# First layer of a two-layer backbone: queries kept in DRAM as rows of channels with both parts of a token block side by side, one store per tile, and requests spaced one tile apart

## The chip, the cores and the metric

The kernel runs on one NeuronCore of a Trainium2 chip. A core has five engines that run their own instruction streams in order and meet at semaphores: PE (TensorE, matrix products; its weight loads, PEld, overlap the products), DVE (VectorE), ACT (ScalarE), POOL (GpSimd) and SP (SyncE, which here issues nearly all transfers). Data lives in DRAM (HBM), in the on-chip memory of 128 partitions, and in PSUM, eight banks into which PE writes. The metric is the device time of one execution in microseconds (us); lower is better.

## The reference, cut to what matters

A backbone of two layers over 1024 latent tokens and 256 context tokens of width 1024. Each layer computes `x += gate * mixer(adaLN(RMSNorm(x)))`; layer 0 mixes by windowed attention with grouped heads (16 query heads, 4 key/value heads, head size 64), layer 1 by multi-head latent attention. What the change touches is the projection of layer 0 and where its queries are kept:

```python
def adaln(cond, w, bias):
    m = jax.nn.silu(cond) @ w + bias
    return jnp.split(m, 3, axis=-1)

def project(h):
    q, k, v, g = jnp.split(h @ w_in, [A_WIDTH, A_WIDTH + A_KV_WIDTH, A_WIDTH + 2 * A_KV_WIDTH], axis=-1)
    ...

qx, kx, vx, gx = project(hx)
qc, kc, vc, gc = project(hc)
qx = apply_rope(qx, cos, sin)
kx = apply_rope(kx, cos, sin)
...
ox = lax.map(attend_block, (qb, kw, vw, mask))
...
yx = (ox * jax.nn.silu(gx)) @ w_out
```

All tensors are fp32. The vectors of adaLN (shift, scale and gate of each layer, for latent and for context tokens) come from products of one conditioning vector with a matrix of 1024 x 3072 per layer.

## The kernel before

**Two parts per number.** An fp32 product is made of three faster ones: every operand is kept as a high part, which ACT makes by a cast (`split`, L120), and a low part, the difference, which DVE or POOL makes (L121); `mm3` (L123–127) issues high x high, low x high, high x low. So L125, L126 and L127 in the profile are the three products of one step.

**The projection of layer 0** (about 100 to 357 us) goes over ten blocks of 256 columns of `a_w_in`, in the order of `blocks`: 0 is V, made earlier; 1, 3, 5 and 6 are queries, 7 is the keys, 2, 4, 8 and 9 are gates. The list `order` (L678–679) has for each of the blocks 1 to 7 one tile of the 256 context tokens (`gp` 0; 48 matmuls of 128x256) and four tiles of 512 latent tokens by 128 columns (`gp` 1 and 2, `c` 0 and 1; 24 matmuls of 128x512); blocks 8 and 9 take the latent tiles first and the context tiles last. One entry of `order` is an *item*. The loop is L747–771. In each item it first calls `fetch` for the block after the current one, then `next_item`, which runs whatever `later(d, fn)` has put off until this item, then some steps of adaLN, and then `proj_t`.

**Weights.** `fetch` (L269–271) calls `load_w` (L222–228): four pieces of 256 KB on SP's queue, each into one of three staging buffers (`stg`), then split by ACT (L120) and POOL (L121) into one of two weight buffers. A fourth piece can be loaded only when the first has been split. The loads of a piece may run far ahead of its split, since nothing but the staging buffer holds them.

**adaLN beside the products.** The remaining adaLN products don't go through PE as matrix products but through DVE: `ada_vec` loads a matrix in 64 pieces of 128x512 (L341, a ring of four buffers), and adds each, scaled by one column of conditioning per partition, to one or two accumulators (L360 for the first piece of a job, L362 for the others; 112 operations in eight jobs). A finished job goes to `ada_sum`: PE sums over partitions (L373), ACT copies the row out of PSUM (L377) or DVE adds a bias (L379). One item later `ada_end` turns the row into columns by four PE transposes (L392), which DVE reads (L167, L170), or stores the row (L385). The loop draws `steps(ada_steps, n)` operations at each item: 2 at a latent tile and 5 at a context tile of a query or key block, 6 at a tile of a gate block, and whatever is left at block 8.

**A query tile** (`proj_t`, L422–492). A latent tile is rotated: DVE multiplies by the cosines (L468) and shuffles (L469), POOL multiplies by the sines (L470) and adds (L472). The rest is done one item later (`rest`): ACT's cast (L120) and DVE's difference (L121) into a staging buffer, then four stores (L487) to `q0_d`, one for each half of the partitions and each part. A context tile has no rotation: cast, difference, four stores (L461). A gate tile is one activation on ACT (L443) and one store (L446, context L448).

**The readback.** `q0_d` is `[4, 64, 2, NT, 512]`: group of four heads, channel, part (high, low), block of 128 tokens, and 512 numbers for four heads of 128 tokens. Attention runs in 40 units of one token block and one group; `prep_q` (L541–548) loads a unit's queries with two transfers (L545), the same rows to both halves of the partitions, in runs of 2 KB. `score` then multiplies by the keys (L569, L570), DVE takes the maximum (L576), ACT the exponential (L579). Other loads on the same queue are the gates (L553) and the output weights (L670).

**Order.** Instructions of one engine run in the order in which the build's scheduler placed them, which follows the program's order and its own estimate of when each can run. So moving a call in the program can move other instructions on the same engine.

Of the kernel before, what the change touches and what calls it, by code (L numbers as in the profile page):

```python
# [9 lines left out]
F32 = mybir.dt.float32  # L10
# [12 lines left out]
NT = TOK // 128  # L23
# [36 lines left out]
def kernel(ctx: ExitStack, tc: tile.TileContext, t, out, dbg=None):  # L60
# [11 lines left out]

    q0_d = dpool.tile([4, 64, 2, NT, 512], F32, name="q0_d")
    g0_d = dpool.tile([8, 128, TOK], F32, name="g0_d")
# [238 lines left out]

    due = []
    item = [0]

    def later(d, fn):
        due.append((item[0] + d, fn))

    def next_item():  # L320
        item[0] += 1
        todo = [x for x in due if x[0] <= item[0]]
        due[:] = [x for x in due if x[0] > item[0]]
        for _, fn in todo:
            fn()

    def ada_vec():
# [18 lines left out]
        for a, cb in jobs:  # L346
# [9 lines left out]
            for k in range(8):  # L356
                w = ws.pop(i)
                for c in range(nw):
                    if k == 0:
                        nc.vector.tensor_scalar_mul(accs[c], w, sc[:, k, c : c + 1])  # L360
                    else:
                        nc.vector.scalar_tensor_tensor(accs[c], w, sc[:, k, c : c + 1], accs[c], ALU.mult, ALU.add)  # L362
# [59 lines left out]
    def proj_t(bi, gp, c):  # L422
        W, c0 = wt[bi], blocks[bi]
        ps = PB[:, 4, :] if (bi, gp) == (9, 0) else pss()
        for cc in (c,) if gp else range(2):
            if gp:
                o = shp(ps, 2, 256)
            elif c0 < 1024:
                o = shp(ps, 2, 2, 128)[:, :, cc, :]
            else:  # L430
                o = ps[:, cc * 256 : cc * 256 + 256]
            for k in range(8):
                if gp:
                    m = [hw[gp][:, :, s, k, :] for s in range(2)]
                elif c0 < 1024:
                    m = [shp(hT[0][:, s, k, :], 2, 128) for s in range(2)]
                else:
                    m = [hT[0][:, s, k, :] for s in range(2)]
# [11 lines left out]
        if gp == 0:  # L450
# [23 lines left out]
        def rest():  # L474
            q = shp(qst.next(), 2, 512)
            if c0 == 1024:
                for e in range(2):
                    es = slice(64 * e, 64 * e + 64)
# [3 lines left out]
                return  # L482
            split(q[:, 0].bitcast(F32R), q[:, 1].bitcast(F32R), a)
            for e in range(2):
                for s in range(2):
                    o0 = e * 256 + c * 128
                    load(  # L487
                        out=q0_d[c0 // 256, :, s, t0 // 128 : t0 // 128 + 4, o0 : o0 + 128],
                        in_=shp(q[64 * e : 64 * e + 64, s], 4, 128),
                    )  # L490

# [15 lines left out]
    ogr = Ring(R, [64, 72], 2048)  # L507
    qtb = [r_at(o, 2, 4, 128) for o in (72, 76, 80, 84, 108)]
    ptr = Ring(R, [88, 92, 96, 100, 104], 1024)
# [17 lines left out]
    class UnitA:  # L527
# [13 lines left out]
        def prep_q(self):  # L541
            i = 4 * ORDER.index(self.ti) + self.g
            self.qT = qtb[i if i < 2 else 2 + (i - 2) % 3]
            for b in range(2):
                load(  # L545
                    out=self.qT[64 * b : 64 * b + 64].bitcast(F32).rearrange("p s h n -> p s (h n)"),
                    in_=q0_d[self.g, :, :, self.ti, :],
                )

# [6 lines left out]
        def score(self, h):  # L556
            g, qT = self.g, self.qT
            P = Pr.next()
            hq = 2 * (h % 2) + h // 2
            self.Ps.append(P)  # L560
# [6 lines left out]
            for i, (po, n, ko, mo) in enumerate(parts):  # L567
                S = pss3()[:, 0:n]
                nc.tensor.matmul(S, qT[:, 0, hq, :], kT[:, g, ko : ko + n], start=True, stop=False)  # L569
                nc.tensor.matmul(S, qT[:, 1, hq, :], kT[:, g, ko : ko + n], start=False, stop=True)  # L570
                prev = sk if mx is None else mx
# [174 lines left out]
    started = {0, 1}  # L746
    for bi, gp, c in order:  # L747
        if bi + 1 < 10 and bi + 1 not in started:
            started.add(bi + 1)
            fetch(bi + 1)  # L750
        next_item()
        steps(ada_steps, 200 if (bi, gp) == (8, 0) else 6 if blocks[bi] >= 1536 else 2 if gp else 5)
        if (bi, gp, c) == (9, 2, 0):
# [16 lines left out]
        if bi >= 8 and gp != 1:  # L770
            for _ in range(2):
                next(wo_fill, None)

    units[1].score(0)
    units[1].score(1)
# [756 lines left out]
```

## Time and profile before

| | us |
|---|---|
| median of three runs | 1643.87 |
| lowest, highest of them | 1639.46, 1645.17 |
| the profiled execution, its own time | 1647.77 |
| its span, first to last instruction | 1645.9 |
| PE busy | 1587.9 |
| DVE, ACT, POOL busy | 964.1, 825.2, 792.5 |
| layer-0 projection after V (blocks 1 to 9) | about 100 to 357 |
| layer-0 attention | about 357 to 750 |
| layer 1 | the rest |

The rows of a timeline are: start in us, length in us, engine, source line, operation, what is written and what is read, how many instructions are joined in the row, and in brackets the idle time before it and what ended that idle time. SPq is SP issuing transfers: its length is that of issuing, not of the transfer. A row of the waits view is: engine, tile and line that waited, what it waited for, then the microseconds in total, how often, and the longest.

### The profile page before, as it was taken

The numbers are of one execution on the slowest core, as the hardware profiler recorded it, in microseconds if no ns is written. First come the engines' busy times: TensorE is split into PE (matmuls) and PEld (weight loads), VectorE is DVE, ScalarE is ACT, GpSimd is POOL, SyncE is SP. The second block draws the span as 40 slices with busy tenths as digits, with TensorE's granted clock in tenths as the row PEclk, the third lists the DMA queues.
The fourth block names the chain that finished last, engine by engine and source line by source line (L and its number), as shares of the span: only waits on it lengthen the run. The fifth ranks groups of instructions, "written<-read, shape, count | busy, mean of one in ns | idle before, by whom it ended". The sixth has DMA issues, their size and how long they took to land.

```text
span 1645.9 us, 23722 instructions
## 1 busy us (share of the span) xinstructions
PE 1587.9 (96%) x8156; PEld 1215.5 (74%) x8156; DVE 964.1 (59%) x1972; ACT 825.2 (50%) x1779; POOL 792.5 (48%) x776
## 2 busy tenths in 40 slices
PE   6899999999999999998999999999999999999998
PEld 2687778887878888878887887566756756666687
DVE  1797853539888888869454015655555455455354
ACT  3622112249777777777333334555555555555421
POOL 1444426224453333345254423686676777668510
PEclk9899999999999999999999999999999999999999
DMA  8557665364343333334127713111111111122151
GB/s 280 165 154 204 180 206 141 94 178 124 93 119 94 91 90 90 90 113 160 52 90 251 222 61 103 61 55 33 39 40 34 45 40 35 49 77 69 47 160 65
DMA packets 127202, 176.75 MB, mean 107 GB/s; under 512 B 11100, under 2 KB 69084, under 8 KB 127080
## 3 DMA queue, kind: packets, MB, share of 16 engines
q1 hardware_dynamic: 124920, 171.12, 34.4%
q10 hardware_dynamic: 2160, 4.11, 0.8%
q8 instruction: 64, 1.05, 0.3%
q14 instruction: 58, 0.48, 0.1%
HBM read 129.04 MB, written 46.15 MB: 106 GB/s over the span
## 4 chain that ended last, share of the span: by engine, by line
PE 70%; DVE 11%; ACT 6%; issue 6%; POOL 3%; DMA 3%; SPq 0%; ACTq 0%; DVEq 0%; POOLq 0%
PE PB L125 15%; PE PB L127 15%; PE PB L126 15%; PE PB L1205 9%; PE PB L1171 4%; PE PB L607 3%; PE PB L597 3%; DVE arena_f L362 2%; DVE arena_r L121 2%; PE PB L569 2%; DVE arena_f L576 1%; PE PB L570 1%; ACT arena_f L579 1%; DMA arena_f<-ada_w 1%; ACT arena_r L120 1%
## 5 line engine op out<-in xcount | busy, mean ns | idle before, releaser
L125 PE MATMUL PB<-arena_r 128*128 128x512 f32 (+3 forms) x1632 | 608.1, 373 | 5.7 <-ACT arena_r L204 3.8
L126 PE MATMUL PB<-arena_r 128*128 128x512 f32 (+3 forms) x1632 | 599.2, 368 | 4.0 <-DVE arena_r L206 3.6
L127 PE MATMUL PB<-arena_r 128*128 128x512 f32 (+3 forms) x1632 | 597.0, 368 | 0.2 <-DVE arena_r L121 0.2
L125 PEld LDWEIGHTS PB<-arena_r 128*128 128x128 f32 (+1 forms) x1632 | 311.2, 191 | 95.3 <-issue 30.3
L1197 POOL TENSOR_TENSOR arena_f<-arena_f 128x512 f32<-128x512 f32 x252 | 326.9, 1297 | 76.4 <-ACT arena_f L1190 61.3
L127 PEld LDWEIGHTS PB<-arena_r 128*128 128x128 f32 (+1 forms) x1632 | 310.9, 191 | 50.3 <-issue 0.9
L126 PEld LDWEIGHTS PB<-arena_r 128*128 128x128 f32 (+1 forms) x1632 | 312.2, 191 | 45.9 <-DVE arena_r L206 4.7
L1190 ACT ACTIVATE arena_f<-PB 128x512 f32<-128x512 f32 x320 | 188.9, 597 | 126.6 <-PE PB L127 114.7
L1175 DVE TENSOR_REDUCE arena_f<-PB 128x1 f32<-128x1280 f32 x128 | 190.5, 1488 | 105.4 <-PE PB L1171 102.9
L121 DVE TENSOR_TENSOR arena_r<-PB,arena_r 128x512 fp32r<-128x512 f32 (+4 forms) x255 | 162.3, 644 | 114.8 <-ACT arena_r L120 113.1
L121 POOL TENSOR_TENSOR arena_r<-arena_f,arena_r 128x512 fp32r<-128x512 f32 x84 | 117.6, 1412 | 153.5 <-ACT arena_r L120 106.5
L120 ACT CAST arena_r<-PB 128x512 fp32r<-128x512 f32 (+4 forms) x255 | 137.7, 549 | 66.6 <-PE PB L597 27.8
L576 DVE CUSTOM_DVE_ANT_0 arena_f<-PB,arena_f,small 128x256 f32<-128x256 f32 (+1 forms) x288 | 145.8, 523 | 28.1 <-PE PB L570 21.9
L1205 PE MATMUL PB<-arena_f 128*64 128x512 f32 x640 | 157.1, 600 | 0.0
L579 ACT ACTIVATE arena_f<-arena_f,small 128x640 f32<-128x640 f32 (+2 forms) x160 | 119.3, 747 | 28.8 <-DVE small L578 27.9
L120 ACT CAST arena_r<-arena_f 128x512 fp32r<-128x512 f32 (+2 forms) x132 | 78.3, 609 | 105.5 <-DMA arena_f<-a_w_in 21.3
L607 PE MATMUL PB<-arena_r 128*128 128x512 f32 x336 | 123.3, 441 | 4.3 <-ACT arena_f L618 3.2
L597 PE MATMUL PB<-ident,arena_f 128*128 128x128 f32 x672 | 110.6, 274 | 1.0 <-ACT arena_f L579 0.8
L1205 PEld LDWEIGHTS PB<-arena_f 128*64 128x64 f32 x640 | 43.5, 136 | 80.9 <-issue 79.7
L1171 PE MATMUL PB<-arena_r 96*128 96x512 f32 (+1 forms) x384 | 99.8, 368 | 2.0 <-DVE arena_f L1175 1.9
L362 DVE SCALAR_TENSOR_TENSOR arena_f<-arena_f,small 128x512 f32<-128x512 f32 x98 | 87.7, 942 | 17.7 <-DMA arena_f<-ada_w 17.5
L597 PEld LDWEIGHTS PB<-ident,arena_f 128*128 128x128 f32 x672 | 83.3, 140 | 19.3 <-ACT arena_f L579 4.7
(149 smaller groups left out, 1768.7 us busy)
## 6 DMA issues: line engine op xcount, KB each, us to landing
arena_r<-q_d SPq DMA_DIRECT2D x80, 256.0 KB
arena_f<-ada_w SPq DMA_DIRECT2D x68, 256.0 KB
arena_f<-a_w_in SPq DMA_DIRECT2D x40, 256.0 KB
q_d<-arena_f SPq DMA_DIRECT2D x80, 128.0 KB
arena_f<-x SPq DMA_DIRECT2D x16, 512.0 KB
qn_d<-arena_f SPq DMA_DIRECT2D x16, 512.0 KB
arena_r<-qn_d SPq DMA_DIRECT2D x32, 256.0 KB
arena_f<-ada_w SPq DMA_DIRECT2D x14, 512.0 KB
```

Source lines behind the costliest of these rows:

```text
L120: nc.scalar.copy(hi, src)
L121: (lo_eng or nc.vector).tensor_sub(lo, src, hi.bitcast(F32))
L125: nc.tensor.matmul(o, ah, bh, start=first, stop=False)
L126: nc.tensor.matmul(o, al, bh, start=False, stop=False)
L127: nc.tensor.matmul(o, ah, bl, start=False, stop=last)
L597: nc.tensor.transpose(pt[:, h, :], self.Ps[h][:, ci * 128 : ci * 128 + 128], ident)
L607: nc.tensor.matmul(self.pv, V[:, self.chunks[ci], self.g, :], PT[:, s], start=ci == 0 and s == 0, stop=ci == self.m - 1 and s == 1,)
L1171: nc.tensor.matmul(psm[:, n0 : n0 + n], self.qT[0:96, 0, b * 128 : b * 128 + 128], kt[0:96, 0, n0 : n0 + n], start=True, stop=True,)
L1175: nc.vector.reduce_max(self.mx[:, 96 + b : 97 + b], psm[:, 0:TOK], AX.X, negate=True)
L1190: nc.scalar.activation(E, S, AF.Exp)
L1197: eng.tensor_add(self.acc, self.acc, E)
L1205: nc.tensor.matmul(self.pv[p : p + 64], Vq[:, c, self.h % 4, :], self.E.pop(c), start=c < 2, stop=c >= NT - 2)
```

## The change

Four things are changed, all in layer 0.

1. `q0_d` becomes `[4, 2, 2, 64, NT, 2, 128]`: group, pair of heads, head in the pair, channel, token block, part, token. The staging buffer has the two parts of each token block side by side, so a latent tile is stored by one transfer of 128 partitions with 4 KB each, and a context tile by two with 2 KB runs. A store is issued one item later than its difference. `prep_q` takes four transfers of 64 partitions, each with two runs of 1 KB, for a unit.
2. `fetch` issues the loads of three pieces at once; the split of the first, the load of the fourth and the splits of the second and third are put off to the next item, the split of the fourth to the one after.
3. The loop calls `next_item` ahead of `fetch`, also in the loop before it (blocks of tokens, `p`), and once more until nothing is put off.
4. `ada_vec` yields once for each piece instead of once for each operation; the load of a further piece and `ada_sum` are put off by one item. The loop draws 2 pieces at an item, and 1 at a latent tile of a query or key block; the drain at block 8 is gone.

```diff
-    q0_d = dpool.tile([4, 64, 2, NT, 512], F32, name="q0_d")
+    q0_d = dpool.tile([4, 2, 2, 64, NT, 2, 128], F32, name="q0_d")
...
-    def fetch(bi, eng=None):
+    def fetch(bi):
         wt[bi] = r_at(wst[bi % 2], 2, 8, 256)
-        load_w(wt[bi], w_in, stg, 8, 256, lo_eng=eng, col0=blocks[bi])
+        src = w_in[:, blocks[bi] : blocks[bi] + 256].rearrange("(k p) n -> p k n", p=128)
+        got = []
+
+        def get(i):
+            got.append(shp(stg.next(), 2, 256))
+            load(out=got[i], in_=src[:, 2 * i : 2 * i + 2, :])
+
+        def cut(i):
+            ks = slice(2 * i, 2 * i + 2)
+            split(wt[bi][:, 0, ks, :], wt[bi][:, 1, ks, :], got[i], nc.gpsimd)
+
+        def second():
+            cut(0)
+            get(3)
+            cut(1)
+            cut(2)
+
+        for i in range(3):
+            get(i)
+        later(1, second)
+        later(2, lambda: cut(3))
...
-                    if c == nw - 1:
-                        fetch_piece(i + 4)
-                    yield
+                later(1, lambda i=i: fetch_piece(i + 4))
+                if k == 7:
+                    later(1, lambda a=a, cb=cb, accs=accs, m=m: ada_sum(a, cb, accs, m))
                 i += 1
-            later(1, lambda a=a, cb=cb, accs=accs, m=m: ada_sum(a, cb, accs, m))
+                yield
...
-                q = shp(qst.next(), 2, 512)
-                split(q[:, 0].bitcast(F32R), q[:, 1].bitcast(F32R), ps)
-                for e in range(2):
-                    for s in range(2):
-                        load(
-                            out=q0_d[c0 // 256, :, s, 0:2, e * 256 : e * 256 + 256],
-                            in_=shp(q[64 * e : 64 * e + 64, s], 2, 256),
-                        )
+                q = shp(qst.next(), 2, 2, 2, 128)
+                u = shp(ps, 2, 2, 128)
+                split(q[:, :, :, 0].bitcast(F32R), q[:, :, :, 1].bitcast(F32R), u)
+
+                def store():
+                    for cc in range(2):
+                        dst = q0_d[c0 // 256, cc, :, :, 0:2].rearrange("e p t s n -> (e p) (t s n)")
+                        load(out=dst, in_=q[:, cc].rearrange("p t s n -> p (t s n)"))
+
+                later(1, store)
...
-            split(q[:, 0].bitcast(F32R), q[:, 1].bitcast(F32R), a)
-            for e in range(2):
-                for s in range(2):
-                    o0 = e * 256 + c * 128
-                    load(
-                        out=q0_d[c0 // 256, :, s, t0 // 128 : t0 // 128 + 4, o0 : o0 + 128],
-                        in_=shp(q[64 * e : 64 * e + 64, s], 4, 128),
-                    )
+            q = shp(qst.next(), 4, 2, 128)
+            split(q[:, :, 0].bitcast(F32R), q[:, :, 1].bitcast(F32R), shp(a, 4, 128))
+            dst = q0_d[c0 // 256, c, :, :, t0 // 128 : t0 // 128 + 4].rearrange("e p t s n -> (e p) (t s n)")
+            later(1, lambda: load(out=dst, in_=q.rearrange("p t s n -> p (t s n)")))
...
             for b in range(2):
-                load(
-                    out=self.qT[64 * b : 64 * b + 64].bitcast(F32).rearrange("p s h n -> p s (h n)"),
-                    in_=q0_d[self.g, :, :, self.ti, :],
-                )
+                for e in range(2):
+                    load(
+                        out=self.qT[64 * b : 64 * b + 64, e].bitcast(F32).rearrange("p c s n -> p c (s n)"),
+                        in_=q0_d[self.g, :, e, :, self.ti].rearrange("c p s n -> p c (s n)"),
+                    )
...
     for bi, gp, c in order:
+        next_item()
         if bi + 1 < 10 and bi + 1 not in started:
             started.add(bi + 1)
             fetch(bi + 1)
-        next_item()
-        steps(ada_steps, 200 if (bi, gp) == (8, 0) else 6 if blocks[bi] >= 1536 else 2 if gp else 5)
+        steps(ada_steps, 1 if gp and blocks[bi] < 1536 else 2)
...
+    while due:
+        next_item()
```

The matmuls on the queries keep their count and size; the context tile's moving operand is one run of 256 columns instead of two of 128.

More of the change, by code (lines that the diff above doesn't have):

```diff
@@ L267, with later, next_item @@
     wt = {}
-    def fetch(bi, eng=None):
-        wt[bi] = r_at(wst[bi % 2], 2, 8, 256)
-        load_w(wt[bi], w_in, stg, 8, 256, lo_eng=eng, col0=blocks[bi])
+    due = []
+    item = [0]
+    def later(d, fn):
+        due.append((item[0] + d, fn))
+    def next_item():
+        item[0] += 1
+        todo = [x for x in due if x[0] <= item[0]]
+        due[:] = [x for x in due if x[0] > item[0]]
+        for _, fn in todo:
+            fn()
+    def fetch(bi):
+        wt[bi] = r_at(wst[bi % 2], 2, 8, 256)
+        src = w_in[:, blocks[bi] : blocks[bi] + 256].rearrange("(k p) n -> p k n", p=128)
[15 more added lines that the diff above has]
+        later(2, lambda: cut(3))
     def fetch0(h):
@@ L311, in ada_cols @@
         ada0.set_cols(mt[:, :, 32:34], 0, h)
[L314 to L325, printed above, removed]
     def ada_vec():
@@ L474, in rest @@
         def rest():
-            q = shp(qst.next(), 2, 512)
             if c0 == 1024:
+                q = shp(qst.next(), 2, 512)
                 for e in range(2):
@@ L507 @@
     ogr = Ring(R, [64, 72], 2048)
-    qtb = [r_at(o, 2, 4, 128) for o in (72, 76, 80, 84, 108)]
+    qtb = [r_at(o, 2, 2, 2, 128) for o in (72, 76, 80, 84, 108)]
     ptr = Ring(R, [88, 92, 96, 100, 104], 1024)
@@ L568, in score @@
                 S = pss3()[:, 0:n]
-                nc.tensor.matmul(S, qT[:, 0, hq, :], kT[:, g, ko : ko + n], start=True, stop=False)
-                nc.tensor.matmul(S, qT[:, 1, hq, :], kT[:, g, ko : ko + n], start=False, stop=True)
+                nc.tensor.matmul(S, q[:, 0], kT[:, g, ko : ko + n], start=True, stop=False)
+                nc.tensor.matmul(S, q[:, 1], kT[:, g, ko : ko + n], start=False, stop=True)
                 prev = sk if mx is None else mx
```

7 lines of the change are left out of this document (2 added, 5 removed).

## The prediction

> **What bounds the kernel now.** I read the page's engine line and its chain of waits first, then the waits of PE by line, then PE's busy time in 20 us windows, and the timelines where a window falls short.
>
> ```profile
> PE 1587.9 (96%) x8156; PEld 1215.5 (74%) x8156; DVE 964.1 (59%) x1972; ACT 825.2 (50%) x1779; POOL 792.5 (48%) x776
> PE PB L392 <- ACT arena_f L377: 7.6, 2, 4.1
> 160.00:180.00 20.00, 20.00 (x96) 15.57 (x95) 19.20 (x29) 2.88 (x5) 5.79 (x4) 1.00 0.84 246
> 180.00:200.00 20.00, 16.57 (x90) 13.16 (x88) 13.64 (x20) 5.47 (x10) 13.59 (x10) 0.99 0.52 134
> 200.00:220.00 20.00, 19.36 (x91) 15.58 (x92) 14.49 (x19) 4.24 (x7) 5.14 (x3) 0.84 0.71 205
> 220.00:240.00 20.00, 16.45 (x75) 13.57 (x74) 10.84 (x17) 2.88 (x5) 3.84 (x3) 0.91 0.78 242
> 240.00:260.00 20.00, 20.00 (x113) 16.35 (x112) 8.25 (x16) 5.46 (x10) 12.58 (x10) 1.00 0.50 129
> 400.00:420.00 20.00, 18.56 (x106) 15.19 (x107) 17.46 (x68) 18.22 (x56) 14.29 (x21) 1.00 0.38 99
> 600.00:620.00 20.00, 19.95 (x119) 16.87 (x118) 17.44 (x61) 15.87 (x38) 7.91 (x11) 1.00 0.30 87
> ```
>
> PE is busy for 96% of the span (the window columns are length, then PE, PEld, DVE, ACT and POOL busy, granted clock, DMA share). In the stage that the change rewrites, the layer-0 projection, PE falls short only in 180–240 us, where the granted clock also falls to 0.84. The waits view names it: two stalls of 7.6 us together, at L392, the transposes that turn a finished adaLN row into columns.
>
> ```profile
> 178.56 0.28 PE L125 MATMUL PB<-arena_r 128*128 128x256 f32 x1
> 187.29 0.39 PE L126 MATMUL PB<-arena_r 128*128 128x512 f32 x1
> 189.56 0.39 PE L127 MATMUL PB<-arena_r 128*128 128x512 f32 x1
> 201.79 0.63 PE L126 MATMUL PB<-arena_r 128*128 128x512 f32 x1
> 206.06 0.61 PE L127 MATMUL PB<-arena_r 128*128 128x512 f32 x1
> 243.82 1.03 PE L373 MATMUL PB<-arena_f,small 128*1 128x512 f32 x4
> 200.64 0.63 PE L392 MATMUL PB<-ident,arena_f 33*128 33x33 f32 x4 [4.07 <-ACT arena_f L377]
> 225.30 0.43 PE L392 MATMUL PB<-ident,arena_f 33*128 33x33 f32 x4 [3.55 <-ACT arena_f L377]
> ```
>
> From 187.29 to 189.56 there are ten steps from one 128x512 matmul to the next: 0.227 us each, so a block tile of 24 takes 5.46 and a context tile of 48 half-width ones about 5.75. Behind the first stall the ten steps from 201.79 to 206.06 take 0.427 each, some 12 at half pace: 12 x 0.2 = 2.4 to 2.5 us of lost clock. To price both stalls with what follows them I count the work between the rows at 178.56 and 243.82: two context tiles, seven block tiles, two L373 groups of 0.96 and two L392 groups of 0.4 make 52.3 us at the full spacing, where 65.3 passed. The stalls cost **13.0 us**: what a build without them can win.
>
> Why are L377's copies late? ACT runs in order, and its copies stand behind a q tile's second half:
>
> ```profile
> 161.08 6.46 DVE L362 SCALAR_TENSOR_TENSOR arena_f<-arena_f,small 128x512 f32<-128x512 f32 x8 [0.77 <-DMA arena_f<-ada_w]
> 167.57 0.69 DVE L121 TENSOR_TENSOR arena_f<-PB,arena_f 128x512 fp32r<-128x512 f32 x1
> 192.73 0.68 DVE L468 TENSOR_TENSOR arena_f<-PB,arena_f 128x512 f32<-128x512 f32 x1
> 195.17 1.28 POOL L470 TENSOR_TENSOR arena_f<-arena_f 128x512 f32<-128x512 f32 x1
> 196.53 1.26 POOL L472 TENSOR_TENSOR arena_f<-arena_f 128x512 f32<-128x512 f32 x1
> 197.82 0.62 ACT L120 CAST arena_f<-arena_f 128x512 fp32r<-128x512 f32 x1 [5.12 <-POOL arena_f L472]
> 199.44 1.15 ACT L377 COPY arena_f<-PB 1x512 f32<-1x512 f32 x2
> 223.55 0.62 ACT L120 CAST arena_r<-arena_f 128x512 fp32r<-128x512 f32 x1 [8.07 <-DMA arena_f<-a_w_in]
> 224.08 1.17 ACT L377 COPY arena_f<-PB 1x512 f32<-1x512 f32 x2
> 218.08 1.61 SPq L227 DMA_DIRECT2D arena_f<-a_w_in  x3
> ```
>
> Stall one: DVE is full (19.20 of 20), so the last q tile of block 3, which PE ends at 178.6, is first touched at 192.73 (L468); L470, L472, the cast at 197.82 and the copy at 199.44 follow. Stall two: a weight piece issued late on SP (218.08) lands at 223.55, its cast holds ACT, and the copy behind it ends at 225.25.
>
> **The change, part by part.** The instruction counts of PE, DVE, ACT and POOL stay; their order moves only in the projection and in the first attention units. In the order of the changed build, 57 of the 112 adaLN steps (L360/L362) stand on DVE ahead of block 3's first q step instead of 64, and 64 ahead of its last tile instead of 80. The finished row's L373/L392 pairs move too: the first pair with an L392, PE-ready at 167 today, is now after block 4's context tile, with one tile of 24 matmuls between L373 and L392.
>
> *When PE gets there.* Today PE starts block 4's context tile at 178.56, runs a block tile and L373 and a second block tile, and reaches an L392 at 200.64 - 4.07 = 196.57, 18.0 later. After the change it has the same without the first block tile, 18.0 - 5.46 = 12.5, and it starts earlier by what left block 3, a group of L373 and one of L392 (0.96 and 0.4): 177.2. So PE reaches the moved L392 at **189.7**.
>
> *When the copy is done.* The fourth weight piece of a block waits on SP until POOL has cut the first. In the changed queue of SP such a piece stands ahead of the adaLN load that DVE's 57th step needs.
>
> ```profile
> 156.19 0.40 SPq L227 DMA_DIRECT2D arena_f<-a_w_in  x1
> 156.68 2.66 SPq L341 DMA_DIRECT2D arena_f<-ada_w  x3
> 160.38 0.62 ACT L120 CAST arena_r<-arena_f 128x512 fp32r<-128x512 f32 x1 [10.36 <-DMA arena_f<-a_w_in]
> 160.90 1.86 SPq L227 DMA_DIRECT2D arena_f<-a_w_in  x2
> 161.07 1.28 POOL L121 TENSOR_TENSOR arena_r<-arena_f,arena_r 128x512 fp32r<-128x512 f32 x1 [10.28 <-ACT arena_r L120]
> 128.54 0.38 SPq L227 DMA_DIRECT2D arena_f<-a_w_in  x1
> 131.43 0.62 ACT L120 CAST arena_r<-arena_f 128x512 fp32r<-128x512 f32 x1 [0.50 <-DMA arena_f<-a_w_in]
> 241.78 0.68 DVE L468 TENSOR_TENSOR arena_f<-PB,arena_f 128x512 f32<-128x512 f32 x1
> 247.54 0.69 DVE L468 TENSOR_TENSOR arena_f<-PB,arena_f 128x512 f32<-128x512 f32 x1
> ```
>
> Today that load goes at 156.68, ahead of the blocked piece (the second of the pair at 160.90), which waits for POOL's cut until 161.07 + 1.28 = 162.35 and is issued by 162.76. After the change the load follows it and two small gate stores, at half a microsecond each 163.5. Today it landed in 4.4 (156.68 to 161.08, where DVE had waited for it); so it lands at 167.9, or 166.5 at the quickest landing here, 128.54 to 131.43. DVE's first q step of block 3 is then at about 168, as today's 167.57: the seven steps taken from ahead of it are lost to a wait, since DVE has nothing else in its order. Behind it come six adaLN steps at 6.46 / 8 = 0.81, so the first tile's L468 is near 173. Tile to tile, the chain L468, shuffle, L470, L472, cast, L121 takes 5.76 (241.78 to 247.54, with DVE otherwise idle): the third tile's L468 is at 184.5, and its L472 ends 4.2 later (0.68, 0.73, 1.28, 1.26 and hand-overs), at 188.7.
>
> On POOL all four weight cuts of block 5 now stand between the third and fourth tile, and the fourth cut's piece is loaded only when the first is done: cut 190, piece issued 190.1, landed 193 by the same 2.9, cast 193.6, cut 194.9, L470 and L472 of the fourth tile 197.5, cast 198.2, the context gate tile's activation 0.6, the two copies 1.15: **200**. PE waits 200 - 189.7, some **10.3 us**; with the ends of each step (the load's landing 2.9 to 5, the first tile 169 to 174.5) 6 to 12. With the 2.5 of lost clock behind it 12.8.
>
> By the Trainium skill, page TensorE: Matmul & The Clock Gate, Part 1, an idle window of about 3.4 us halves the clock and 3.4 us of work restore it. That would be 1.7 us of loss, an estimate from the page, where this trace has 2.4 to 2.5: by the page the stall costs 12.0.
>
> *The other pairs.* The second (stall two's kind) has L373 after block 4's last tile and L392 after block 5's context tile, 5.75 later; on ACT its copies stand behind a weight cast whose load SP no longer holds back with four q stores. Today the copies are 3.55 late after one tile; with two or three microseconds of SP's issuing gone and the longer tile I put them between 4 early and 1 late, cost 0: stall two goes. The third falls behind block 5's last q tile on ACT: copy done between 2 us early and 2.5 late; I take 0.7. The next stands on ACT behind the issue of the mask's load, which waits for a k tile's DVE step: that step follows PE's tile by up to one chain of 5.76, while PE has one tile of 5.46 and the wait for the copies themselves (1.15) and the L373 group: 0 to 6, I take 3.5, without a clock term since the shortest idle shown with one is 3.55. **Sum: 12.8 + 0.7 + 3.5 = 17.0 against 13.0: +4.0 us.**
>
> *Stores and readback.*
>
> ```profile
> L545 SPq DMA_DIRECT2D arena_r<-q_d x80: 512/518/1221, 349.3 to 690.8; - x80
> L487 SPq DMA_DIRECT2D q_d<-arena_f x64: 574/607/892, 114.0 to 289.9; - x64
> 349.95 2.62 SPq L545 DMA_DIRECT2D arena_r<-q_d  x2
> 357.62 0.28 PE L569 MATMUL PB<-arena_r 128*128 128x256 f32 x1
> ```
>
> 64 tile stores become 16: 48 x 0.607 = 29 us of SP issuing saved over 176 us, where SP mostly waits for buffers, not for issue slots; on the path 0 to -2, I take 0, since the steps above wait for POOL and DVE. Context stores fall from 16 to 8, likewise. A tile's store now goes one item later; the staging buffer it reads has two places, a q tile each: 0. The readback grows from 80 to 160 issues of 0.518, so one unit's loads end 1.04 us later. The tightest unit, the first, has its last issue done at 349.95 + 2.62 = 352.57 and its first matmul at 357.62: 5.05 of cover, 4.0 after the change, against landings of 2.9 to 4.4 above. So 0 to 0.4 there, and I take 0; later units are loaded while earlier ones compute. Without the cover, a unit would pay its landing, 2.9 to 4.4. Behind 360 us PE's order is the same but for the first ten units, and PE is busy 19.95 of 20 at 600: what the projection gains or loses stays to the end; those ten units, while PE is below 19 of 20, as in 400–420 still, I bound at -2 to +2 (a tenth of a window's length).
>
> **The rivals.** *Both stalls go.* If the load or the cuts come ten microseconds sooner than worked out, the copy is done before 189.7 and all 13.0 come back: 1631. For it: 16 fewer adaLN steps ahead of the last tile, worth 16 x 0.81 = 13 us of DVE. Against: the chain, not DVE's work, then sets the tiles. *Only stall two goes*: the moved one stays at 4 + 2.5, 6.5 won: 1637; it needs the copy at 194. *Slower*: the same place, SP's blocked piece and POOL's cuts ahead of the fourth tile, at the upper ends, and the later pairs with it: 12 + 2.5, 2.5, 6 + 2.5, together 25.5, less 13.0: +12.5, 1656.4. It decides when the moved copy is done after 201. *The readback is late*: at the slowest issue four loads take 4 x 1.22 = 4.9, and with a landing of 2.9 to 4.4 up to 9.3 where the first unit has 357.62 - 349.95 = 7.7; half a microsecond at each of the first ten units, before PE has a lead, is +5 on top of the forecast: 1652.9. By the Trainium skill, page DMA: Bandwidth & Descriptors, Anatomy of one DMA, each transfer has some 2 us of fixed cost, which speaks against four small loads for two: four in a row are 8 us, by estimate 0.3 late a unit, +3 in all; no run here shows it yet. *No effect*, the order's moves cancelling out, is inside the forecast's range.
>
> **How the numbers follow.** The profiled execution took 1647.77 (span 1645.9), 3.9 over the runs' median; the differences are put on the median: 1643.87 + 4.0 = **1647.9**. A measurement of this kernel tells about 0.3% (4.9 us) from no change: below 1639.0 is faster, above 1648.8 slower. Chances: forecast 0.45 (its own range 1640 to 1654; 0.01 faster, 0.25 the same, 0.19 slower); both stalls go 0.18 (0.17, 0.01, 0); only one goes 0.14 (0.05, 0.09, 0); slower 0.17; readback 0.06 (0, 0.01, 0.05). Faster 0.23, same 0.36, slower 0.41. The range, 1635 to 1660, leaves out most of the first rival.
>
> **What would show it.** Right: one PE wait of 6 to 12 us at the transposes after block 4's first block tile, near 190, on the copy; none near 222; the adaLN load behind the blocked weight piece on SP, and POOL's four cuts between block 3's third and fourth tiles. Wrong: no wait at the transposes; a wait on q_d in the attention; a first q step of block 3 near 160, not 167.

## The result and the profile after

| | before | after |
|---|---|---|
| median of five runs on one chip | 1643.87 | 1651.63 |
| lowest, highest | 1639.46, 1645.17 | 1649.72, 1652.03 |
| profiled execution, its span | 1647.77, 1645.9 | 1651.76, 1649.9 |

After to before is 1.0051, with a 95% interval of 1.0035 to 1.0067: 7.8 us between the medians, slower by more than the 0.3% that a measurement tells. The forecast was +4.0.

After's engine line and its wait at the transposes (now L415, on the copies at L400):

```profile
PE 1588.0 (96%) x8156; PEld 1213.0 (74%) x8156; DVE 953.8 (58%) x1972; ACT 826.4 (50%) x1779; POOL 790.9 (48%) x776
...
PE PB L415 <- ACT arena_f L400: 13.1, 2, 10.5
```

PE's own work is the same, 1588.0 to 1587.9. The two stalls, 7.6 before, are now 13.1, and one of them is 10.5. After's windows, with the columns of the prediction's:

```profile
160.00:180.00 20.00, 20.00 (x106) 17.27 (x105) 9.26 (x16) 1.35 (x3) 4.80 (x4) 1.00 0.55 180
180.00:200.00 20.00, 9.53 (x48) 7.08 (x48) 6.99 (x13) 6.17 (x11) 12.51 (x10) 0.77 0.39 133
200.00:220.00 20.00, 20.00 (x82) 15.43 (x81) 8.96 (x17) 4.49 (x8) 3.98 (x4) 0.89 0.63 187
220.00:240.00 20.00, 20.00 (x112) 17.35 (x112) 14.59 (x25) 2.06 (x4) 5.23 (x4) 1.00 0.63 197
300.00:320.00 20.00, 17.40 (x73) 14.12 (x72) 14.35 (x23) 7.06 (x12) 9.34 (x7) 0.91 0.28 88
```

Before, PE ran below 20 in 180–200, 200–220 and 220–240. Now the whole stall lies in 180–200 (9.53, clock 0.77, then 0.89 while it recovers), 220–240 is full, and there is a new hole in 300–320. DVE, which was full in 160–180 (19.20), has 9.26 there: it waits instead of working. The three stages are bounded by the first row-sum matmul (L373, now L396) and by the first and last score product (L569, now L587). The rows give how many, the shortest, median and longest in ns, then the first and last start. Before:

```profile
L373 PE MATMUL PB<-arena_f,small x28: 590/591/592, 125.2 to 285.9; 128*1 128x512 f32 x28
...
L569 PE MATMUL PB<-arena_r x288: 274/283/443, 357.6 to 716.3; 128*128 128x256 f32 x144
```

After:

```profile
L396 PE MATMUL PB<-arena_f,small x28: 590/591/592, 124.3 to 350.1; 128*1 128x512 f32 x28
...
L587 PE MATMUL PB<-arena_r x288: 274/283/446, 362.0 to 723.1; 128*128 128x256 f32 x143, 128*128 128x384 f32 x1
```

| stage of the span | before | after | difference |
|---|---|---|---|
| up to the first row sum | 125.2 | 124.3 | -0.9 |
| projection, to the first score product | 232.4 | 237.7 | +5.3 |
| attention, to the last score product | 358.7 | 361.1 | +2.4 |
| the rest, to the end of the span | 929.6 | 926.8 | -2.8 |

The four add up to +4.0, the difference of the two spans and the very sum that was predicted; but that is partly chance. In the fourteen profiles of this study, the rest, whose code no kernel here changes, takes 926.2 to 929.6, and the stretch up to the first row sum 122.1 to 125.2: the profiled execution of before has the longest of both. The projection and the attention alone make 5.3 + 2.4 = 7.7, what the medians show (7.8). Below, "projection" and "attention" are these two stages, read from the same rows of each profile.

### The profile page after: what moved, and what is told of

Its sections match the earlier page's. It is cut to its first block, busy times and chain, and to the rows that moved or that the text cites. A ratio compares the mean times of both kernels' runs of the same rounds, so it can differ in the third digit from the quotient of the medians.

```text
span 1649.9 us, 23797 instructions
## 1 busy us (share of the span) xinstructions
PE 1588.0 (96%) x8156; PEld 1213.0 (74%) x8156; DVE 953.8 (58%) x1972; ACT 826.4 (50%) x1779; POOL 790.9 (48%) x776
## 4 chain that ended last, share of the span: by engine, by line
PE 66%; DVE 10%; issue 8%; ACT 7%; POOL 6%; DMA 2%; ACTq 0%; SPq 0%; POOLq 0%; DVEq 0%
PE PB L126 13%; PE PB L128 13%; PE PB L127 13%; PE PB L1226 9%; PE PB L1192 4%; PE PB L625 4%; PE PB L615 3%; DVE arena_r L122 2%; PE PB L587 2%; DVE arena_f L385 2%; PE PB L588 2%; DVE arena_f L594 1%; POOL arena_f L491 1%; POOL arena_r L122 1%; ACT arena_r L121 1%
## 5 line engine op out<-in xcount | busy, mean ns | idle before, releaser
L648 POOL TENSOR_TENSOR arena_f<-arena_f 128x256 f32<-128x256 f32 x39 | 28.7, 737 | 135.2 <-ACT arena_f L636 135.2
```

## The experiments

| kernel | median | ratio to before beside it (95%) | projection | attention |
|---|---|---|---|---|
| before (its profile) | 1643.87 | | 232.4 | 358.7 |
| after | 1651.63 | 1.0051 (1.0035–1.0067) | 237.7 | 361.1 |
| E1 before, again | 1645.23 | 0.9998 (0.9987–1.0008) | 232.3 | 358.4 |
| E2 after, columns two items later | 1641.39 | 0.9971 (0.9961–0.9982) | 227.6 | 360.6 |
| E3 before, columns two items later | 1632.19 | 0.9917 (0.9902–0.9931) | 219.9 | 359.1 |
| E4 before with the steps part alone | 1654.94 | 1.0053 (1.0039–1.0068) | 243.9 | 359.0 |
| E5 before with the layout alone | 1637.83 | 0.9965 (0.9951–0.9978) | 226.3 | 360.7 |
| E6 after, two loads a unit | 1648.28 | 1.0028 (1.0018–1.0039) | 237.9 | 359.8 |
| E7 after, fourth piece issued by POOL | 1658.09 | 1.0088 (1.0073–1.0102) | 244.4 | 360.9 |
| E8 E3 and a loop at the end | 1630.91 | 0.9925 (0.9911–0.9939) | 220.0 | 358.8 |
| E9 after, a fourth staging buffer | 1642.53 | 0.9985 (0.9972–0.9999) | 230.4 | 360.8 |
| E10 before, layout, two loads, columns one item later | 1632.93 | 0.9919 (0.9904–0.9933) | 220.7 | 358.7 |
| E11 before, columns one item later | 1638.72 | 0.9955 (0.9941–0.9969) | 226.1 | 359.0 |
| E12 after, two loads, columns two items later | 1638.05 | 0.9949 (0.9934–0.9965) | 227.9 | 358.5 |

**E1: the kernel before, once more.** No edit.

> The kernel before, unchanged, profiled and timed a second time. The two profiled executions differ by 4.0 us (1647.77 and 1651.76), the medians by 7.8. If the two waits at the transposes are of fixed length, this profile shows 4.1 and 3.5 us again, a time near 1644 and a ratio of 1.000. If their length varies from execution to execution (rival), they come out some us shorter or longer, and the time moves with them by about the same amount; then the 3.8 us by which the medians went further apart than the profiles lie in these waits.

1645.23 beside 1645.6, and the same two stalls (4.20 and 3.66). Its profile, 1644.54 with a span of 1642.8, has the same projection and attention as before's own, to 0.3, and 927.7 behind them: the 929.6 belongs to one execution, not to the kernel.

**E2 and E3: the columns later.** If the whole cost of the projection is PE waiting for the copies, putting the transposes off must win it back, in either kernel.

```diff
-        later(1, lambda: ada_end(a, cb, m, n))
+        later(3, lambda: ada_end(a, cb, m, n))
```

> The changed kernel with the transposes three items behind the row sum instead of one, so that PE does two more tiles (10.9 us) ahead of them. Theory (the copy at 198.9 is late, PE waits 10.5 and then 2.6, with 2.5 and 1.7 of lost clock behind them): both waits go, 17 us are won, 1634 or a little more, since PE reaches the transposes at 200.3, only 1.4 after the copy. Rival (the queries' readback of 160 transfers sets the attention's start): the wait at the transposes goes and comes back at the first score products, near 357, and the time stays above 1645.

> The kernel before with the transposes three items behind the row sum. Theory: both waits go, 13.0 us by the profile of before, 1631; if the waits of the timed runs are shorter than those of that profile, by 4 us less, 1635. Rival (the projection is also bound by DVE, 19.2 of 20 us busy in 160-180): the wait moves to the products and less than 6 us are won, 1638 or more.

In E3, and in E8, the gate bias of a later job is written into the buffer of one finished row of layer 1's adaLN before that row is turned into columns, so these adaLN values differ; the counts of instructions are the same. E3's projection is 219.9 and has no stall: that is the full pace here. So before loses 12.5 to its two stalls (worked out: 13.0) and after 17.8 (worked out: 17.0). E2 wins 10.1 of the 17.8 back, where 17 were expected; one wait at L415 is left, of 2.1, and others come up in the key block, of 1.36 on DVE and 0.89 on POOL. Off the transposes, after is still not at the pace of E3.

**E4 and E5: the parts alone.** E4 is before with the drawing of steps and the putting off within `ada_vec`; E5 is before with the layout, its stores and its loads. The spacing of the weight requests and the call ahead of `fetch` were not tried alone.

```diff
-                    if c == nw - 1:
-                        fetch_piece(i + 4)
-                    yield
+                later(1, lambda i=i: fetch_piece(i + 4))
+                if k == 7:
+                    later(1, lambda a=a, cb=cb, accs=accs, m=m: ada_sum(a, cb, accs, m))
                 i += 1
-            later(1, lambda a=a, cb=cb, accs=accs, m=m: ada_sum(a, cb, accs, m))
+                yield
...
-        steps(ada_steps, 200 if (bi, gp) == (8, 0) else 6 if blocks[bi] >= 1536 else 2 if gp else 5)
+        steps(ada_steps, 1 if gp and blocks[bi] < 1536 else 2)
```

> The kernel before with the adaLN steps of the change alone (one yield for a piece, 2 or 1 at an item, loads and sums put off by one item), queries and weights as before. Theory (the new place of the transposes and the load behind the blocked weight piece make the loss): one wait of 9 to 12 us near 190 at the transposes, and a time of 1650 to 1656. Rival (the new queries' layout makes the loss): a time within 3 us of 1644.

E5 takes from the change what the diff above shows of `q0_d`, the stores and the loads, with what reads them:

```diff
-    q0_d = dpool.tile([4, 64, 2, NT, 512], F32, name="q0_d")
+    q0_d = dpool.tile([4, 2, 2, 64, NT, 2, 128], F32, name="q0_d")
...
+            later(1, lambda: load(out=dst, in_=q.rearrange("p t s n -> p (t s n)")))
...
-    qtb = [r_at(o, 2, 4, 128) for o in (72, 76, 80, 84, 108)]
+    qtb = [r_at(o, 2, 2, 2, 128) for o in (72, 76, 80, 84, 108)]
...
-            hq = 2 * (h % 2) + h // 2
+            q = qT[:, h % 2, h // 2]
```

> The kernel before with the new layout of the queries alone (one store per tile one item later, four readback transfers a unit); weights and adaLN steps as before. So far: the attention from the first to the last score product takes 358.4 to 359.1 us in three kernels with the old layout and 360.6 to 361.1 in two with the new one. Theory (the 80 added transfers, or where they make the build's scheduler put things, cost the attention some 2 us): attention 360.5 to 361.2 and the two waits at the transposes as before, 1646 to 1649 where before has 1645. Rival (the 48 stores fewer free SP and shorten the waits in the projection): 1640 to 1644. Rival (the layout costs nothing, the 2 us come from the new adaLN steps): attention near 358.7 and 1645.

The waits at the transposes, first of E4, then of E5:

```profile
PE PB L392 <- ACT arena_f L377: 17.9, 2, 9.6
```

```profile
PE PB L392 <- ACT arena_f L377: 2.9, 1, 2.9
```

The steps part alone is slower than before by about what the whole change is, and its projection is the longer by 11.5: two long stalls, at 198.36 and 308.40. Near 222 it has none; its L392 there follows without a wait, as it does in E5:

```profile
225.08 0.44 PE L392 MATMUL PB<-ident,arena_f 33*128 33x33 f32 x4
```

The layout alone is faster, as the first rival has it and by more than it said: the second stall is gone, the first falls from 4.1 to 2.9. That +11.5 and -6.1 make +5.4 in the projection, where the change has +5.3, is chance: the stalls are others (9.6 and 8.3 in E4, 10.5 and 2.6 in after), and E4's profiled execution, 1658.19, lies 3.3 above its median. By the medians the parts are +9.3 and -6.5, together +2.8, where the change has +7.8. What makes the rest, the parts not tried alone or the parts acting on each other, is not shown.

**E6: two loads a unit.** The new rows, read by two transfers of 64 partitions as before.

```diff
-                for e in range(2):
-                    load(
-                        out=self.qT[64 * b : 64 * b + 64, e].bitcast(F32).rearrange("p c s n -> p c (s n)"),
-                        in_=q0_d[self.g, :, e, :, self.ti].rearrange("c p s n -> p c (s n)"),
-                    )
+                load(
+                    out=self.qT[64 * b : 64 * b + 64].bitcast(F32).rearrange("p c e s n -> p (c e) (s n)"),
+                    in_=q0_d[self.g, :, :, :, self.ti].rearrange("c e p s n -> p (c e) (s n)"),
+                )
```

> The changed kernel with the two transfers of a half joined into one (the on-chip buffer ordered as in DRAM), so two readback transfers a unit with four runs of 1 KB each, as many as before the change. Theory (the number of transfers costs the attention 2 us): attention 358.5 to 359.2, the wait of 10.5 at the transposes stays, and the time is 2 to 3 us below that of the changed kernel, a ratio near 1.0035. Rival (the shorter runs cost it): attention stays at 360.6 to 361.1, ratio near 1.005.

The projection keeps its loss (237.9, stalls of 10.7 and 2.4); the attention falls to 359.8, half of the way back and short of the expected 358.5 to 359.2. E10 and E12 below, with the same two loads, are all the way back (358.7 and 358.5).

**E7 and E9: the piece that SP waits for.** E7 lets POOL issue the fourth piece of a block, so that SP need not stand before it; E9 takes one buffer from the tiles' ring of five and gives it to the staging ring, so that a fourth piece needs no cut first.

```diff
-            load(out=got[i], in_=src[:, 2 * i : 2 * i + 2, :])
+            (nc.gpsimd.dma_start if i == 3 else load)(out=got[i], in_=src[:, 2 * i : 2 * i + 2, :])
```

```diff
-    stg = Ring(F, [4, 6, 8], 512)
+    stg = Ring(F, [4, 6, 8, 46], 512)
...
-    ev = Ring(F, [38, 40, 42, 44, 46], 512)
+    ev = Ring(F, [38, 40, 42, 44], 512)
```

> The changed kernel with the fourth weight piece of each block issued by POOL, which makes the cut that it waits for, instead of SP. Theory (the adaLN load behind the blocked piece makes block 3's first q step late, and the chain from there sets the copy): the load that was issued at 162.8 goes near 158, DVE's first q step comes at 162 instead of 167.7, the copy 5 to 6 us earlier, the wait at the transposes falls from 10.5 to 4 to 6 and the time by 4 to 6 us, a ratio of 1.001 to 1.003. Rival (the four cuts between the third and fourth q tile alone set it): the first q step comes earlier, the wait stays at 9 or more.

> The changed kernel with four staging buffers for weight pieces instead of three (one taken from the five of the tiles), so that no piece waits for the first cut of its own block; the order on PE, DVE and ACT is the same. Theory (a piece that waits for POOL's cut holds SP, and with it the adaLN load, and later the cut ahead of the fourth q tile): the load that was issued at 162.8 goes by 159, block 3's first q step comes near 162 instead of 167.7, the four cuts run without the wait for their last piece, the copy is done near 192, and the wait at the transposes falls from 10.5 to 3 to 5; a time 5 to 7 us below the changed kernel, ratio 1.000 to 1.002. Rival (the steps' new order on DVE sets it whatever the queues do): a wait of 9 or more and a ratio near 1.005.

Rows of E9's timelines (the adaLN load on SP, DVE's first q step of block 3, POOL's cuts of block 5, the copies), then its wait:

```profile
154.64 2.27 SPq L364 DMA_DIRECT2D arena_f<-ada_w  x4
159.87 0.69 DVE L122 TENSOR_TENSOR arena_f<-PB,arena_f 128x512 fp32r<-128x512 f32 x1
179.65 5.48 POOL L122 TENSOR_TENSOR arena_r<-arena_f,arena_r 128x512 fp32r<-128x512 f32 x4
188.77 1.15 ACT L400 COPY arena_f<-PB 1x512 f32<-1x512 f32 x2
```

```profile
PE PB L415 <- ACT arena_f L400: 5.5, 2, 3.7
```

With the blocked piece gone, the load is issued 8.2 us sooner than in after (154.64 for 162.81). The whole stage starts 2.1 sooner in this profile (its first row sum at 122.2 for 124.3), so 6.1 of them are the edit's. The first q step follows (159.87 for 167.69), the four cuts run in one go, the copies end at 189.92 instead of 198.84, 6.8 sooner by the stage's own start, and the stall falls from 10.5 to 3.65, also 6.8: 7.3 of the projection's time go (237.7 to 230.4), nearly all of it at that one place (the second wait is 1.81 for 2.60). E7 settles nothing: its adaLN load came only 2.1 sooner (160.67), 1.3 of that from an earlier start of the stage (123.0 for 124.3), and the fourth piece, issued by POOL at 187.32, was cut at 192.32, so the stall became 11.3 and a second one of 6.8 came up.

**E8.** E3 with this behind the loop:

```diff
+    while due:
+        next_item()
```

> The kernel before with the transposes three items behind the row sum and the loop's last put-off steps done after it, so that the last gate rows are stored as well, which the earlier version of this left out. Both theories: the same time as that version, 1632, a ratio of 0.991 to 0.993.

Nothing was left over at the loop's end, so the lines issue nothing: E8 is a second timing of E3, and gives the same (220.0).

**E10, E11 and E12: what is kept of the change.** E11 is before with this edit; E10 is E5 with this edit and E6's two loads; E12 is E2 with E6's two loads.

```diff
-        later(1, lambda: ada_end(a, cb, m, n))
+        later(2, lambda: ada_end(a, cb, m, n))
```

> The kernel before with the new layout, two readback transfers a unit, and the transposes two items behind the row sum; weights and adaLN steps as before. Theory: no wait at the transposes, so the projection takes 220 us, the attention 359.5 to 360 as with two joined transfers, 1630 to 1632, a ratio of 0.991 to 0.993. Rival (another stall takes the place of the removed ones): a ratio above 0.995.

> The kernel before with the transposes two items behind the row sum, nothing else. Theory: PE does one more tile (5.46 us) ahead of each, more than either wait (4.1 and 3.5), so both go: 1630 to 1633, ratio 0.991 to 0.993, and the new layout is then worth nothing. Rival (the layout's fewer stores still help once the waits are gone): 3 us or more above the run with the layout.

> The changed kernel with the transposes three items behind the row sum and two readback transfers a unit. Theory: as with the late transposes alone (ratio 0.997), and 1 to 2.5 us less for the readback: ratio 0.995 to 0.9965; the small waits near 290 to 310 in the key block stay, so that it is 5 us or more above the old steps with late transposes. Rival (the new steps cost nothing once the transposes are late): a ratio of 0.992 to 0.993.

E10 has no stall, 220.7 in the projection and 358.7 in the attention: 0.9919 of before, faster than both kernels, and within 2 us of E3 and E8, whose adaLN values differ. Without the layout (E11) one stall of 2.65 is left where none was expected, and why is on ACT's and SP's timelines of E11:

```profile
218.30 0.62 ACT L120 CAST arena_r<-arena_f 128x512 fp32r<-128x512 f32 x1 [12.65 <-DMA arena_f<-a_w_in]
```

```profile
213.41 1.63 SPq L227 DMA_DIRECT2D arena_f<-a_w_in  x3
```

A weight piece is issued late on SP, lands, and its cast holds ACT ahead of the copies: stall two of before. With the layout, whose stores are fewer, the pieces are issued at 211.33 and the stall is gone (E10). E12, with the whole change kept, has the old attention (358.5) but not the full pace in the projection (227.9): what is left of the change costs 7 to 8 us there that the later columns don't return.

## Why the prediction was right, and where it was not

**The moved stall: right, by its own steps.** SP, DVE, POOL, ACT and PE of after:

```profile
155.03 1.93 SPq L292 DMA_DIRECT2D arena_f<-a_w_in  x3
...
161.64 0.37 SPq L292 DMA_DIRECT2D arena_f<-a_w_in  x1
...
162.81 1.78 SPq L364 DMA_DIRECT2D arena_f<-ada_w  x4
...
188.85 0.38 SPq L292 DMA_DIRECT2D arena_f<-a_w_in  x1
```

```profile
166.91 0.75 DVE L385 SCALAR_TENSOR_TENSOR arena_f<-arena_f,small 128x512 f32<-128x512 f32 x1 [6.96 <-DMA arena_f<-ada_w]
167.69 0.69 DVE L122 TENSOR_TENSOR arena_f<-PB,arena_f 128x512 fp32r<-128x512 f32 x1
...
172.28 0.68 DVE L489 TENSOR_TENSOR arena_f<-PB,arena_f 128x512 f32<-128x512 f32 x1
```

```profile
186.29 1.29 POOL L493 TENSOR_TENSOR arena_f<-arena_f 128x512 f32<-128x512 f32 x1
187.53 4.18 POOL L122 TENSOR_TENSOR arena_r<-arena_f,arena_r 128x512 fp32r<-128x512 f32 x3
192.82 1.26 POOL L122 TENSOR_TENSOR arena_r<-arena_f,arena_r 128x512 fp32r<-128x512 f32 x1 [1.10 <-ACT arena_r L121]
...
195.38 1.26 POOL L493 TENSOR_TENSOR arena_f<-arena_f 128x512 f32<-128x512 f32 x1
```

```profile
196.67 0.62 ACT L121 CAST arena_f<-arena_f 128x512 fp32r<-128x512 f32 x1 [3.93 <-POOL arena_f L493]
...
197.69 1.15 ACT L400 COPY arena_f<-PB 1x512 f32<-1x512 f32 x2
```

```profile
198.89 0.64 PE L415 MATMUL PB<-ident,arena_f 33*128 33x33 f32 x4 [10.47 <-ACT arena_f L400]
...
200.04 0.63 PE L127 MATMUL PB<-arena_r 128*128 128x512 f32 x1
...
203.88 0.61 PE L127 MATMUL PB<-arena_r 128*128 128x512 f32 x1
```

Read from the top: SP takes three pieces and stands before the fourth until 161.64, so the adaLN load goes out at 162.81 (predicted 163.5; two stores of half a microsecond behind 162.76 would have made 163.8, and the two took 0.62 together). DVE sits 6.96 for it and takes its first q step at 167.69 (168), the first tile at 172.28 (173). POOL makes three cuts, waits for the fourth piece, which SP could issue only at 188.85 (190.1), cuts it at 192.82 and is done with the tile at 196.64 (197.5). The copies end at 198.84 (200), and PE had come at 198.89 - 10.47 = 188.42 (189.7). Each step is about a microsecond early, both ends alike, since after's first row sum is 0.9 earlier than before's; so the wait is 10.47 for the 10.3 worked out. From 200.04 to 203.88 nine steps take 0.427 each, where 0.227 is the full pace: the 2.5 of lost clock stand. The Trainium skill, page TensorE: Matmul & The Clock Gate, Part 1, has some 3.4 us of work to restore the clock; here it came back 5.4 us after PE resumed (198.89 to 204.31), so the trace's loss and not the 1.7 estimated from the page was the one to use. E9 shows that the blocked pieces on SP made 6.8 of the 10.47, 5.7 of it by the first q step already; that was only argued before.

**Stall two: right, with one of its reasons misread.** No wait near 222, PE full in 220–240. The prediction gave two reasons, the fewer stores on SP and the longer tile ahead of the transposes. The second misreads the rows: before has block 5's context tile at this place too, between the row sum and the transposes that PE reached at 225.30 - 3.55 = 221.75:

```profile
214.78 1.03 PE L373 MATMUL PB<-arena_f,small 128*1 128x512 f32 x4
215.74 0.39 PE L125 MATMUL PB<-arena_r 128*128 128x256 f32 x1
```

The first is borne out: with the stores and without the new steps (E5) the stall is gone. But E4, with the new steps and the old stores, doesn't wait there either. So the fewer stores are enough and not needed; in both the weight cast ahead of the copies hardly waits for its piece, 0.21 in E5 and 0.16 in E4, where it held ACT for 8.07 before.

**The next pair: the step "without a clock term" failed.** After's ACT and PE:

```profile
301.22 0.33 ACTq L773 DMA_DIRECT2D arena_f<-mask  x1
...
301.60 1.18 ACT L400 COPY arena_f<-PB 1x512 f32<-1x512 f32 x2 [1.85 <-DVE arena_f L489]
```

```profile
302.83 0.43 PE L415 MATMUL PB<-ident,arena_f 33*128 33x33 f32 x4 [2.60 <-ACT arena_f L400]
...
303.68 0.63 PE L127 MATMUL PB<-arena_r 128*128 128x512 f32 x1
...
306.24 0.63 PE L127 MATMUL PB<-arena_r 128*128 128x512 f32 x1
```

The place and the reason are as put: the copies stand behind the issue of the mask's load, which waits for a k tile on DVE. The wait is 2.60, within 0 to 6 and under the 3.5 taken, but some eight steps at half pace follow it, 1.6 to 1.7 more: 4.3 for 3.5. The clock falls after shorter idles than the 3.55 that before showed. The third pair (0.7 taken) has no wait. Summed, 10.47 + 2.5 + 4.3 = 17.3 of stalls; the stage loses 17.8 against E3, 12.5 before. So the term of the projection was +4.0 and measured +5.3, most of the difference being that before's two stalls cost 12.5 and not 13.0 and that after has some 0.5 outside its stalls.

**Stores taken at 0: mis-sized when alone.** "0 to -2, I take 0, since the steps above wait for POOL and DVE" holds only under the steps part. On the kernel before, the layout is worth 232.4 - 226.3 = 6.1 of the projection (E5), because there stall two hung on SP's queue. In the whole change most of the same gain is inside "stall two goes", so the sum did not miss it.

**Readback taken at 0: this is the step that failed.** The bound of -2 to +2 for the first attention units was nearly the right size, but the value taken was not: +2.4. The attention takes 360.6 to 361.1 in all five kernels with four transfers a unit (after, E2, E5, E7, E9), 358.4 to 359.1 in all with the old layout, and 358.5 to 359.8 with two joined ones (E6, E10, E12). The transfers that read and write `q_d`, in after's view of that tensor (the last row is of all of them together):

```profile
L563 SPq DMA_DIRECT2D arena_r<-q_d x160: 573/580/1687, 352.3 to 698.2; - x160
L507 SPq DMA_DIRECT2D q_d<-arena_f x16: 326/332/1216, 115.7 to 292.9; - x16
...
DMA to landing us min/median/max: 2.3/2.8/4.6
```

One issue takes 0.580, where the same 0.518 as before was assumed, and a store of a whole tile 0.332 for the 0.607 of one of the four before. But the rival that the readback is late did not come: the first unit has from 352.3 to its first score product at 362.0, against landings of at most 4.6, and no wait of PE on `q_d` stands in the list of waits. The page DMA: Bandwidth & Descriptors of the Trainium skill (Anatomy of one DMA) gives some 2 us of fixed cost for a transfer that POOL issues, and says that most of it is the wait for completion. The landings here, 2.3 and more for transfers that SP issues, are of that size or somewhat more, but the costs of four in a row don't add up to the estimated 8 us: the first unit's four are issued by 354.98 and no landing that the trace shows is longer than 4.6, so that all are in by 359.6. What is lost lies in PE's busy time early in the stage. The first 40 us from the first score product, before and then after:

```profile
357.60:397.60 40.00, 38.18 (x251) 32.12 (x249) 34.11 (x137) 36.72 (x90) 12.48 (x17) 1.00 0.56 147
```

```profile
362.00:402.00 40.00, 37.06 (x240) 30.65 (x239) 31.21 (x130) 34.68 (x83) 10.64 (x14) 1.00 0.48 145
```

That is eleven matmuls fewer and 1.1 less of busy PE. After also has a wait which before lacks, of the output product for the high part of a unit's gated result, which POOL writes, twice, 0.9 each:

```profile
PE PB L126 <- POOL arena_r L652: 1.7, 2, 0.9
```

It stands in E2, E7 and E9 too and not in E6, E12 or E5, though E5 loses as much. The order of the instructions, read from the fourteen traces, says more. In all nine kernels with two transfers a unit, of the old layout or the new (before, E1, E3, E4, E6, E8, E10, E11, E12), PE, DVE, ACT and POOL run the same sequence from the first to the last score product. With four transfers the sequence is another, the same in after, E2, E7 and E9 and a third one in E5, until about the 425th matmul of PE. So the two added transfers made the build's scheduler place the early units differently, and wherever the attention takes 360.6 or more, that order is changed. Whether the order costs the time, or the added issue time on SP (160 of 0.580 for 80 of 0.518), these runs don't separate, since the two always come together; it stays open. The runs of 1 KB alone are not it, since E10 and E12 have them. The 1.3 between E6 and E12, whose order is the same, is something else: it arises in the first 24 us of the stage (the 151st matmul comes at 23.9 in E6 and 22.6 in E12), and its cause is open too.

**What decided.** By medians the change is +7.8, and the profiles put +5.3 of it in the projection and +2.4 in the attention. The mechanism of the first was right, the second was put at nothing; the forecast of +4.0 is half of what came.

## What to carry to other kernels

Where a transfer waits on a queue for a buffer, count what stands behind it: here one blocked weight piece delayed a load by 6 us and cost 7 us on PE, and one more buffer or a consumer one item later was worth more than a better spacing of the requests. A change in parts should be timed in parts: the layout alone won 0.35%, the spacing of the steps lost 0.53%, and the two together hid that the first was worth keeping. When a sum agrees with one pair of profiles, look at the stages that the change doesn't touch before believing it.

## What the hardware showed beyond what was expected

How long PE must idle before the clock falls is no fixed number here. After idles of 2.60 (after), 2.65 (E11) and 2.89 (E5) half pace follows at once; after 3.55 in before it begins 2.0 us after PE resumed (225.30, half pace from 227.27); after 2.12 in E2 it begins 1.7 us after PE resumed (300.08, half pace from 301.76), and after 1.81 in E9 as well (293.35, from 295.09); after the same 2.12 in E12 it does not come at all. Most of these idles are under the 3.4 us that the page TensorE: Matmul & The Clock Gate of the Trainium skill gives for an idle window (Part 1); the measurement decides, and a stall of two microseconds or more may cost as much again.
